# Filling the first stretch of a two-layer transformer kernel: TensorE matmuls on a tile of ones, packed inputs, a split transpose of x

## The chip, the core and the metric

The kernel runs on one core of a Trainium2 chip. A core has a matrix engine (TensorE, in the profile PE for its matmuls and PEld for its weight loads), a vector engine (VectorE, DVE), a scalar engine (ScalarE, ACT), a general engine (GpSimd, POOL) and a queue engine (SyncE, SP) that issues most of the DMAs. Each engine works through its own list of instructions in order, and waits by semaphores for the others. Matmul results land in eight PSUM banks; everything else lies in SBUF. The metric is device time in microseconds (us) for one execution; lower is better.

## The reference, cut to what matters

A row of conditions `c` makes shifts, scales and gates for every sublayer; x is 256 tokens by 1024. Two layers of three sublayers each (FFN, attention, FFN) follow:

```python
c_act = jax.nn.silu(c)
for layer in range(2):
    mod = (c_act @ ada_w[layer] + ada_b[layer]).reshape(B, 3, 3, 1024)
    h = rmsnorm(x, g) * (1 + mod[:, 0, 1]) + mod[:, 0, 0]
    x = x + 0.5 * mod[:, 0, 2] * swiglu(h, w13, w2)      # FFN, inner width 2816
    ...                                                  # attention: layer 0 windowed with sinks (swa),
    ...                                                  # layer 1 with forget gates (fox); then a second FFN
```

All inputs are float32. The modulation weights `ada_w` are 2 x 1024 x 9216 and are read whole, as are the weights of the FFNs and the projections.

## The kernel before

Precision is kept by splitting: each weight tile `wraw` (128 x 1024) is rounded on ACT to `whi` (fp32r), and DVE writes the remainder `wlo`. The activations `hT` and `gT` are split in the same way, and `mm3` issues three fast matmuls (hi*hi, hi*lo, lo*hi) for each product. The modulation `c_act @ ada_w` isn't done on PE: `cb` is silu(c) spread over all 128 partitions, and one DVE instruction (`dot`) multiplies a tile of `ada_w` with it and sums along the row.

Order on the engines is not the order of the code. A recorder keeps all operations with their dependences, and a planner (`Recorder.run`) then walks through simulated time with a cost for each operation, and takes for every engine the ready operation that is due first. DMAs have a simulated rate (343 bytes per ns in the code), matmuls a cost that doubles while the simulated TensorE clock is cold. The result is emitted as a fixed list per engine. `rec.also` gives an operation a second engine that it may be put on.

The first stretch is `start`. Conditions `c` and x are loaded, ACT takes the silu of the row `crow` (the first partition of `gate`), two matmuls with a row of ones spread it (`ps<-gate,ones`), and ACT copies the result to `cb`. `rstd` takes the sums of squares of x, `norm` scales it to `xn`, 16 transposes on PE (`ps<-ident,xn`) turn it, and ACT copies it to two tiles `xT`. Then come 8 steps, one for each 128 rows k of the first w13 matrix (`w13s`): `modulated(k)` makes two dots, shift and scale of this k, and `h`, hi and lo of `hT`; 24 matmuls (N=512) for four column chunks c follow, into all eight PSUM banks (`pa` and `ps` in the profile). The lines that spread silu(c) and the two alternatives for `h`:

```python
A.activation(crow, crow, AF.Silu)
for i in range(2):
    T.matmul(pc, ones[0:1, :], crow[:, i * 512 : i * 512 + 512], start=True, stop=True)
    A.copy(cb[:, i * 512 : i * 512 + 512], pc)
...
o = V.tensor_scalar(out=t, in0=xT[k // 4][:, k % 4, :], scalar1=mod[1][:, k : k + 1], ...)
rec.also(o, A, "activation", t, xT[k // 4][:, k % 4, :], AF.Identity, ...)
```

Small inputs come by five DMAs: `colb` and `gcol` (issued by ACT), `qkg`, `sink` and `bf` (issued by POOL, the last two spread over the partitions by the DMA). Every instruction is emitted from one helper line, so the profile's line is the same for all, and names of tiles tell them apart.

## Time and profile before

| what | us |
|---|---|
| median of 3 runs | 1003.95 (1002.23 to 1004.24) |
| the profiled execution: its own time | 1004.72 |
| its span, first to last instruction | 1002.9 |
| PE busy in the span | 981.6 (98%) |
| DVE / ACT / POOL busy | 774.7 / 522.5 / 55.3 |
| PE busy in the first 15.74 us | 7.69 |
| first split matmul of step 0 starts at | 15.74 |
| attention of layer 0, 205 to 276: PE busy | 66.36 of 71.00 |
| attention of layer 1, 680 to 790: PE busy | 106.77 of 110.00 |

PE is in use almost throughout, so a reader looks for the places where it waits: the first 15.74 us, the two attention stages and the tail. Busy time in the profile includes the pipeline's latency, so that a row of short matmuls looks fuller than it is.

### The profile page before, as it was taken

To read this page: it belongs to the slowest core of one execution; us is meant where nothing else is said; L and a number is where in the kernel's file an instruction comes from. 1 tells how busy PE (TensorE), PEld (TensorE's weight loads), DVE (VectorE), ACT (ScalarE), POOL (GpSimd) and SP (SyncE) were. 2 spreads that over 40 slices of the span, in tenths; PEclk is the share of its full clock that TensorE was granted. 3 is DMA by queue.
4 is the path that set the end of the run, shared out by engine and by line. 5 is a ranking of instruction groups with operands and counts; after the bars stand their busy time and mean duration, and the time that the engine had idled before them with its cause. 6 is when DMAs were issued, how large, how long until landed. Compare 5 with 4: busy or idle time off the path is not lost.

```text
span 1002.9 us, 16605 instructions
## 1 busy us (share of the span) xinstructions
PE 981.6 (98%) x6262; PEld 891.2 (89%) x6262; DVE 774.7 (77%) x1396; ACT 522.5 (52%) x946; POOL 55.3 (6%) x77
## 2 busy tenths in 40 slices
PE   6999999998999999999999999999999999999997
PEld 4898999897788899999889999989899789999996
DVE  5999788888999976677897767678788997555532
ACT  6473335465986543454544433447577675444420
POOL 1000000033000000000100000002211010000000
PEclk9999999999999999999999999999999999999999
DMA  9999899779446886786787878844536357656501
GB/s 344 409 354 399 332 391 308 253 269 294 148 150 253 330 316 225 318 302 237 283 315 275 311 274 306 317 157 153 166 128 249 137 191 263 212 191 240 189 33 64
DMA packets 74258, 252.92 MB, mean 252 GB/s; under 512 B 8497, under 2 KB 11969, under 8 KB 74178
## 3 DMA queue, kind: packets, MB, share of 16 engines
q1 hardware_dynamic: 73186, 249.63, 67.9%
q10 hardware_dynamic: 896, 2.21, 0.7%
q8 instruction: 49, 0.80, 0.3%
q0 software_dynamic: 96, 0.02, 0.1%
q14 instruction: 31, 0.25, 0.1%
HBM read 249.95 MB, written 1.88 MB: 251 GB/s over the span
## 4 chain that ended last, share of the span: by engine, by line
PE 91%; ACT 3%; DVE 3%; DMA 1%; POOL 1%; issue 1%; DVEq 0%; POOLq 0%
PE ps L238 57%; PE pa L238 33%; ACT t L238 1%; POOL qrs L238 1%; DVE wraw L238 1%; DMA sink<-in_sink 1%; DMA M<-foxsc 1%; DVE wlo L238 1%; ACT zeroed L238 0%; DVE qss L238 0%; DVE t L238 0%; ACT whi L238 0%; DVE qn L238 0%; ACT hT L238 0%; DVE qkv L238 0%
## 5 line engine op out<-in xcount | busy, mean ns | idle before, releaser
L238 DVE TENSOR_TENSOR wlo<-wraw,whi 128x1024 fp32r<-128x1024 f32 (+2 forms) x328 | 379.8, 1180 | 96.1 <-ACT whi L238 45.4
L238 ACT CAST whi<-wraw 128x1024 fp32r<-128x1024 f32 (+2 forms) x328 | 325.4, 1021 | 164.1 <-PE ps L238 74.5
L238 PE MATMUL ps<-hT,whi 128*128 128x256 f32 x2176 | 393.0, 283 | 0.0
L238 PEld LDWEIGHTS ps<-hT,whi 128*128 128x128 f32 x2176 | 341.0, 192 | 2.6 <-issue 0.6
L238 PE MATMUL ps<-hT,wlo 128*128 128x256 f32 x1088 | 307.7, 283 | 0.0
L238 PE MATMUL pa<-whi,gT 128*128 128x512 f32 x704 | 217.9, 391 | 0.3 <-DVE gT L238 0.3
L238 PEld LDWEIGHTS ps<-hT,wlo 128*128 128x128 f32 x1088 | 208.7, 192 | 0.0
L238 PE MATMUL ps<-whi,hT 128*128 128x384 f32 (+2 forms) x640 | 188.0, 365 | 1.4 <-DVE zeroed L238 1.4
L238 DVE SCALAR_TENSOR_TENSOR wraw<-wraw,cb 128x1024 f32<-128x1024 f32 x144 | 173.2, 1217 | 6.8 <-DMA wraw<-in_ada 6.8
L238 PEld LDWEIGHTS pa<-whi,gT 128*128 128x128 f32 x704 | 132.2, 188 | 27.7 <-DVE gT L238 0.7
L238 PE MATMUL pa<-wlo,gT 128*128 128x512 f32 x352 | 133.4, 391 | 0.0
L238 PEld LDWEIGHTS ps<-whi,hT 128*128 128x128 f32 x640 | 117.9, 189 | 12.8 <-DVE zeroed L238 1.8
L238 PE MATMUL ps<-wlo,hT 128*128 128x384 f32 (+2 forms) x320 | 116.6, 365 | 0.5 <-DVE wlo L238 0.5
L238 ACT ACTIVATE sil<-ps 128x256 f32<-128x256 f32 x84 | 31.8, 381 | 105.7 <-PE ps L238 105.7
L238 PEld LDWEIGHTS pa<-wlo,gT 128*128 128x128 f32 x352 | 66.1, 188 | 12.8
L238 PEld LDWEIGHTS ps<-wlo,hT 128*128 128x128 f32 x320 | 60.5, 189 | 6.5 <-DVE wlo L238 0.9
L238 DVE TENSOR_TENSOR sil<-sil,ps 128x256 f32<-128x256 f32 x84 | 34.6, 415 | 39.0 <-ACT sil L238 39.0
L238 ACT CAST gT<-sil 128x256 fp32r<-128x256 f32 x68 | 27.0, 405 | 61.1 <-DVE sil L238 54.2
L238 DVE TENSOR_TENSOR gT<-sil,gT 128x256 fp32r<-128x256 f32 x68 | 28.2, 421 | 18.8 <-ACT gT L238 18.8
L238 POOL TENSOR_TENSOR rs<-u,mhalf 128x1 f32<-128x1 f32 x12 | 14.5, 1209 | 484.5 <-DVE u L238 484.5
L238 PE MATMUL pa<-whi,OT 128*128 128x512 f32 x128 | 39.4, 392 | 0.0
L238 PE MATMUL pa<-zeroed 128*128 128x256 f32 x192 | 37.2, 300 | 2.2 <-ACT zeroed L238 1.8
(120 smaller groups left out, 732.2 us busy)
## 6 DMA issues: line engine op xcount, KB each, us to landing
wraw<-in_ada SPq DMA_DIRECT2D x144, 512.0 KB, 7.1
wraw<-in_w13b SPq DMA_DIRECT2D x132, 512.0 KB, 6.5
wraw<-in_w SPq DMA_DIRECT2D x88, 512.0 KB, 5.9
wraw<-in_w13a SPq DMA_DIRECT2D x28, 512.0 KB, 7.9
wraw<-in_fwin SPq DMA_DIRECT2D x28, 384.0 KB, 4.3
wraw<-in_w13s SPq DMA_DIRECT2D x16, 512.0 KB, 10.2
wraw<-in_swin SPq DMA_DIRECT2D x16, 384.0 KB, 7.2
wraw<-in_swout SPq DMA_DIRECT2D x8, 512.0 KB, 6.3
```

The lines of the kernel that those rows point to most:

```text
L238: return lambda: getattr(real, method)(*[un(v) for v in a], **{n: un(v) for n, v in k.items()})
```

## The change

Seven edits, all but one of them in the first stretch:

1. 48 filler matmuls: stationary `ones` (128 x 128), moving 64 columns of the same tile, float32, into a PSUM bank `warm` that nobody reads. The planner emits the next filler whenever PE would have nothing to issue at that moment, and they cost what its price for a float32 matmul says.
2. The simulated DMA rate goes from 343 to 400 bytes per ns, in due times and in the simulated transfers. This touches the order of the whole program.
3. The five small inputs become one tensor `small` (128 x 232), with one DMA on ACT's queue.
4. silu moves from the row to the spread copy: the matmuls take the raw `c`, and ACT applies Silu as it evacuates each half of `cb`.
5. In `start`, the sums of squares may go to DVE (`first=True`), and `xn` is always made on DVE.
6. x is transposed in two halves: columns 0 to 511 before step 0, columns 512 to 1023 inside step 0, after the first column chunk.
7. `h` of the 8 steps is made on ACT alone.

```diff
+    ones = cp.tile([P, P], F32, name="ones")
+    G.memset(ones, 1.0)
+    warm = psum()
+    rec.filler = True
+    for _ in range(NWARM):
+        T.matmul(warm[:, 0:64], ones, ones[:, 0:64], start=True, stop=True)
+    rec.filler = False
...
+                    if pick is None and e == "PE" and fillers and fillers[0].wait == 0 and t >= fillers[0].ready:
+                        o = fillers.pop(0)
+                        busy[e] = t + o.dur * (2 if cold else 1)
...
-                due = min(due, s.due - o.dur - lat(o, s) - (DMARG + o.bytes / 343 if o.bytes else 0))
+                due = min(due, s.due - o.dur - lat(o, s) - (DMARG + o.bytes / 400 if o.bytes else 0))
...
-    A.activation(crow, crow, AF.Silu)
-        A.copy(cb[:, i * 512 : i * 512 + 512], pc)
+        A.activation(cb[:, i * 512 : i * 512 + 512], pc, AF.Silu)
...
+            if first:
+                rec.also(o, V, "scalar_tensor_tensor", out=t, in0=x[h][:, c], scalar=1.0 / 1024.0, in1=x[h][:, c],
+                         op0=ALU.mult, op1=ALU.mult, accum_out=ss[:, dh : dh + 1])
...
-        xn = [norm(0), norm(1, A)]
+        rs = [rstd(h, True) for h in range(2)]
+        def transposed_x(g):
+            for h in range(2):
+                V.tensor_scalar(out=xn, in0=x[h][:, g * 512 : g * 512 + 512], scalar1=rs[h], scalar2=None, op0=ALU.mult)
+                ...
+        transposed_x(0)
...
-            o = V.tensor_scalar(out=t, in0=xT[k // 4][:, k % 4, :], ...)
-            rec.also(o, A, "activation", ...)
+            A.activation(t, xT[k // 4][:, k % 4, :], AF.Identity, scale=mod[1][:, k : k + 1], bias=mod[0][:, k : k + 1])
...
+                if k == 0 and c == 1:
+                    transposed_x(1)
```

What stands on PE from its first instruction to the first split matmul (`pa<-...`), before:

```order
L238 MATMUL ps<-gate,ones 128x512 x2
L238 MATMUL ps<-ident,xn 128x128 x16
L238 MATMUL pa<-whi,hT_212 128x512
L238 MATMUL pa<-wlo,hT_212 128x512
L238 MATMUL pa<-whi,hT_216 128x512
```

and after:

```order
L240 MATMUL ps<-ones 128x64 x8
L240 MATMUL ps<-gate,ones 128x512 x2
L240 MATMUL ps<-ones 128x64 x16
L240 MATMUL ps<-ident,xn 128x128 x4
L240 MATMUL ps<-ones 128x64 x3
L240 MATMUL ps<-ident,xn 128x128 x4
L240 MATMUL ps<-ones 128x64 x21
L240 MATMUL pa<-whi,hT_232 128x512
L240 MATMUL pa<-wlo,hT_232 128x512
L240 MATMUL pa<-whi,hT_232 128x512
L240 MATMUL pa<-wlo,hT_232 128x512
L240 MATMUL pa<-whi,hT_245 128x512 x2
```

All 48 fillers (`ps<-ones`) stand ahead of the first split matmul: 8 ahead of the spreading of c, 16 ahead of the first transposes, 3 between the two groups of transposes, 21 behind them. Eight transposes have left this place; they stand behind the sixth split matmul.

ACT's list in the same stretch, before:

```order
L238 ACT_TABLE_LOAD
L238 ACTIVATE gate<-gate 1x1024
L238 ACTIVATE t,ss<-x_94 128x512
L238 ACTIVATE t,ss<-x_99 128x512
L238 COPY cb<-ps 128x512
L238 ACTIVATE t,ss<-x_99 128x512
L238 ACTIVATE t,ss<-x_94 128x512
L238 COPY cb<-ps 128x512
L238 ACTIVATE xn<-x_99,rs 128x512 x2
L238 CAST whi<-wraw 128x1024
```

and after:

```order
L240 ACT_TABLE_LOAD
L240 ACTIVATE t,ss<-x_94 128x512
L240 ACT_TABLE_LOAD
L240 ACTIVATE cb<-ps 128x512 x2
L240 COPY xT<-ps 128x4x128
L240 CAST whi<-wraw 128x1024
L240 COPY xT<-ps 128x4x128
L240 ACTIVATE h_226<-xT,mod_203,mod_187 128x256
L240 CAST hT_232<-h_226 128x256
L240 CAST whi<-wraw 128x1024
L240 COPY xT<-ps 128x4x128 x2
L240 CAST whi<-wraw 128x1024 x2
```

Three of the four squares and both `xn` have gone to DVE, a second table load stands ahead of the two Silu, and the copies of the second half of `xT` stand ahead of the casts of step 1's weights.

Beyond the first stretch PE's list differs in the attention of layer 0 (205 to 276 us of the profile). Around its first scores (`ps<-qkv`; `ident,kn` and `ident,qn` are transposes of normalised keys and queries), before:

```order
L238 MATMUL ps<-qkv 128x128 x3
L238 MATMUL ps<-qkv 128x256 x3
L238 MATMUL ps<-whi,hT_2185 128x384
L238 MATMUL ps<-qkv 128x128 x3
L238 MATMUL ps<-qkv 128x256 x3
L238 MATMUL pa<-ident,kn 128x128
L238 MATMUL pa<-ident,qn 128x128 x2
L238 MATMUL ps<-wlo,hT_2185 128x384
```

and after:

```order
L240 MATMUL pa<-ident,qn 128x128 x2
L240 MATMUL pa<-ident,kn 128x128
L240 MATMUL ps<-whi,hT_2269 128x384
L240 MATMUL ps<-wlo,hT_2269 128x384
L240 MATMUL ps<-whi,hT_2309 128x384
L240 MATMUL ps<-qkv 128x128 x3
L240 MATMUL ps<-qkv 128x256 x3
L240 MATMUL ps<-qkv 128x128 x3
L240 MATMUL ps<-qkv 128x256 x3
L240 MATMUL ps<-whi,hT_2244 128x384
```

The transposes that stood right behind the first scores now stand ahead of them, with projection matmuls (`ps<-whi,hT`) between.

## The prediction, made before the changed kernel ran

> **What bounds the kernel now.** I read the page's busy shares first, then a table of windows by stage, then the chain that ended last.

> ```profile
> PE 981.6 (98%) x6262; PEld 891.2 (89%) x6262; DVE 774.7 (77%) x1396; ACT 522.5 (52%) x946; POOL 55.3 (6%) x77
> 0.00:15.74 15.74, 7.69 (x20) 4.30 (x20) 5.33 (x15) 11.28 (x21) 4.37 (x15) 1.00 0.88 306
> 15.74:23.02 7.28, 7.28 (x25) 5.89 (x26) 7.28 (x12) 5.01 (x7) 0.00 (x0) 1.00 1.02 407
> 23.02:61.10 38.08, 38.08 (x170) 31.53 (x170) 36.37 (x66) 17.97 (x27) 0.00 (x0) 1.00 1.03 409
> 61.10:205.00 143.90, 143.90 (x962) 132.50 (x962) 123.73 (x187) 68.05 (x104) 1.72 (x2) 1.00 0.91 336
> 205.00:276.00 71.00, 66.36 (x423) 58.94 (x422) 64.52 (x193) 50.04 (x146) 19.61 (x30) 0.98 0.67 226
> ```

> A window's row gives its length and the busy time of PE, PEld, DVE, ACT and POOL, then the granted clock. PE never stops from 15.74 to 205 us. So what the first stretch gains or loses is carried to 205 unchanged, provided DVE and the DMAs (GB/s in the last column) keep up; and PE idles 8.05 us (15.74 - 7.69) ahead of it. The chain shows what filled that time.

> ```profile
> 2.41 6.77 DMA sink<-in_sink
> 12.74 1.07 ACT xT L238 x2
> 15.74 4.53 PE pa L238 x12
> 20.28 2.74 PE ps L238 x12
> 23.02 2.72 PE pa L238 x12
> 55.66 2.72 PE pa L238 x12
> ```

> A slow small DMA (sink, 6.77 us) held DVE's list, behind which stood rstd; then xn, transposes, xT, h. Step 0 is 24 matmuls: the first 12 took 4.53 us, the next 2.74, all later dozens 2.72, or 0.227 each. The first stretch therefore ends at 23.02 for step 0, and every later step costs 5.44.

> **The clock.** PE's rows show why the first dozen is slow.

> ```profile
> 4.14 3.75 PE L238 MATMUL ps<-gate,ones 1*128 1x512 f32 x4 [4.14 <-ACT gate L238]
> 10.95 2.82 PE L238 MATMUL ps<-ident,xn 128*128 128x128 f32 x12 [3.06 <-ACT xn L238]
> 18.04 1.05 PE L238 MATMUL pa<-whi,hT 128*128 128x512 f32 x2
> 18.90 0.46 PE L238 MATMUL pa<-wlo,hT 128*128 128x512 f32 x1
> 237.00:238.00 1.00, 0.50 (x2) 0.42 (x2) 1.00 (x3) 0.99 (x4) 1.00 (x1) 0.74 1.14 259
> 238.00:239.00 1.00, 1.00 (x4) 1.00 (x4) 1.00 (x4) 0.44 (x2) 0.69 (x2) 0.50 0.75 164
> 241.00:242.00 1.00, 1.00 (x9) 0.77 (x7) 1.00 (x2) 0.97 (x3) 0.62 (x1) 1.00 0.98 393
> ```

> Up to 18.90 two matmuls take 0.86 us from start to start, 0.43 each; the one at 18.90 is already shorter, and the later dozens take 0.227 each. So the clock doubles at about 19.0, 3.3 us after full matmuls began. The granted clock column says 1.00 there and doesn't show this early half clock; at 237.5 it does show a fall to 0.50, for some 3.4 us. Neither the 3.75 us on c (one row of the array) nor the transposes raised it.

> **The fillers.** Each is a float32 matmul with a full stationary tile. The nearest rows are three such instructions with 16 moving columns, at full clock:

> ```profile
> 702.34 0.74 PEld L238 LDWEIGHTS ps<-lf,tri 128*128 128x128 f32 x6
> L238 PEld LDWEIGHTS ps<-lf,tri x6: 187/192/192, 702.3 to 702.9; 128*128 128x128 f32 x6
> 211.10 1.03 PE L238 MATMUL ps<-ident,xn 128*128 128x128 f32 x8
> 211.89 0.42 PE L238 MATMUL ps<-whi,hT 128*128 128x384 f32 x1
> 0.74 0.20 POOL L238 MEMSET ones<- 128x128 f32 x1 [0.29 <-POOLq L1272]
> ```

> Three instructions make six weight loads and six matmuls; the loads start (0.74 - 0.19)/5 = 0.11 us apart. So a filler (two of each) is 0.22 us at full clock, 0.44 at half. That is a lower bound as 64 columns stream longer than 16; if loads and matmuls didn't overlap it would be about 0.33. I take 0.22, since weight loads overlap the matmuls everywhere else (PE 98% and PEld 89% busy). Eight transposes take 0.79 (211.10 to 211.89), the spreading of c half of 3.75, or 1.88, all at full clock. PE's list up to the first split matmul is then 48 x 0.22 + 1.88 + 0.79 = 13.23 us at full clock. It can start at 1.0, when `ones` is written. If the clock rises at time w, the part before w runs at half speed, so the first split matmul starts at S = 1.0 + 13.23 + (w - 1.0)/2.

> For w the earliest is 1.0 + 3.3 = 4.3 (fillers count like full matmuls). The first 8 fillers last 8 x 0.44 = 3.5 us, to 4.5, and then come the matmuls on c, of the kind that didn't raise the clock before. I take 6.0, nearer to the early end as the fillers use all 128 rows, and later than 4.3 because that 3.75 us stretch shows that length alone isn't enough. S = 16.73.

> [...]

> **Is anything later than PE's list?**

> ```profile
> 1.64 1.28 ACT L238 ACT_TABLE_LOAD   x1 [1.64 <-PEq L1272]
> 4.85 0.63 ACT L238 ACTIVATE t<-x 128x512 f32<-128x512 f32 x1 [0.85 <-DMA x<-in_x]
> 6.79 0.63 ACT L238 ACTIVATE t<-x 128x512 f32<-128x512 f32 x1 [1.22 <-DMA x<-in_x]
> 9.57 1.09 POOL L238 TENSOR_TENSOR rs<-u,mhalf 128x1 f32<-128x1 f32 x2 [5.38 <-DVE u L238]
> 12.24 1.22 DVE L238 SCALAR_TENSOR_TENSOR wraw<-wraw,cb 128x1024 f32<-128x1024 f32 x1
> 14.64 0.61 ACT L238 ACTIVATE h<-xT,mod,mod 128x256 f32<-128x256 f32 x1
> 15.29 0.40 ACT L238 CAST hT<-h 128x256 fp32r<-128x256 f32 x1
> 16.59 1.05 ACT L238 CAST whi<-wraw 128x1024 fp32r<-128x1024 f32 x1
> ```

> x lands at 4.85 and 6.79; two squares on DVE (half of 1.22 each) end at 8.0, rs (0.55) at 8.8, two xn at 9.6. PE's 8 fillers end at 4.52, c's matmuls run at half clock to 6.0 and need (3.75 - 1.48)/2 = 1.14 more, to 7.14, and 16 fillers end at 10.7: the transposes don't wait. ACT: square to 5.6, the added table load (1.28) to 6.9, two Silu like the copies of xT (0.53 each), done by 8. The table load is hidden under x and c; without that cover it would cost its 1.28. Dots 2 x 1.15 from 9.6 end at 11.9, shift and scale 12.2, second xT copy 12.7, h and hT 13.8. So the data are ready near 14 and wait for PE: 21 fillers of 0.22 (4.6 us) stand ahead of them. The packing removes the sink wait (up to 9.2), and one DMA on ACT's queue replaces five on two; both gains end in the same wait for PE's list, so I count them as zero.

> **Step 0 and the later steps.** Step 0 lasts 24 x 0.227 + 0.79 for the moved transposes = 6.23, and ends at 16.73 + 6.23 = 22.96, against 23.02: -0.06. The two moved xn come on DVE before the second `wlo`; ACT's xT copies wait for the transposes, and behind them are queued the casts of step 1 and its h.

> ```profile
> 24.91 0.41 DVE L238 TENSOR_SCALAR h<-xT,mod,mod 128x256 f32<-128x256 f32 x1
> 27.90 1.22 DVE L238 SCALAR_TENSOR_TENSOR wraw<-wraw,cb 128x1024 f32<-128x1024 f32 x1
> 33.49 1.22 DVE L238 SCALAR_TENSOR_TENSOR wraw<-wraw,cb 128x1024 f32<-128x1024 f32 x1
> 11.47 1.61 SPq L238 DMA_DIRECT2D wraw<-in_w13s  x2
> 14.04 1.61 SPq L238 DMA_DIRECT2D wraw<-in_ada  x2
> ```

> Transposes end near 19, copies 20, two casts of 1.05 at 22, h and hi 22.9: just ahead of step 1 at 22.96. DVE needs 5.59 us per step (27.90 to 33.49), more than PE's 5.44; without h (0.33 to the next start) it needs 5.26. So edit 7 earns nothing by itself, but keeps DVE ahead. Lo of hT now stands behind both `wlo`, and I add 0.2 for stalls in steps 2 and 3 (0 to 0.5). A pair of tiles is issued every 2.57 us, a step's four in 5.14, less than 5.44: DMAs don't bind.

> **The attention of layer 0** is reordered by edit 2; its waits are these:

> ```profile
> 236.19 0.33 PE L238 MATMUL pa<-ident,kn 128*128 128x128 f32 x1 [0.62 <-ACT kn L238]
> 237.58 0.69 PE L238 MATMUL ps<-wlo,hT 128*128 128x384 f32 x1 [0.50 <-DVE wlo L238]
> 248.37 0.44 PE L238 MATMUL ps<-whi,hT 128*128 128x384 f32 x1 [1.45 <-DVE zeroed L238]
> ```

> With kn's and qn's transposes now ahead of the scores, the waits of 0.62 and 0.50 can go, and the clock's fall behind them. DVE (64.52 of 71.00) limits that gain. I take half of 1.12, -0.56; bounds are -3 (both waits, 1.45, and part of the slow clock) and +2 (the same size in new waits). The rest of the program keeps PE's order: 0.

> The sum: -0.06 + 0.2 - 0.56 = -0.4 us, on the profiled execution 1004.72 to 1004.3, on the median 1003.95, 0.77 below it, to 1003.5. About 0.2%, or 2 us, is what a measurement of this kernel can tell from no change.

> **The rivals.**

> 1. The clock rises late: slower. If c's matmuls interrupt the count, it starts anew in the second batch, at 4.52 + 3.75 = 8.3, and w is 11.6 or later, 13 with some delay: S = 20.2, step 0 ends at 26.5, 3.5 later than in the forecast: 1007.0. It decides from w = 10.8, where S is 2.4 us later and the sum reaches +2. If fillers never count, all runs at half clock: S = 1.0 + 26.5 = 27.5, step 0 as before 7.28 plus 1.6 for the transposes at half clock, 36.4 against 23.02: 1017. For it: two kinds of PE work did not raise the clock. Against: fillers use all rows, as the matmuls at 15.74 do.

> 2. Attention recovers more: faster. If the fall of the clock at 237.5 doesn't come back, 3.4 us at half speed give up to 1.7 us, and with the waits of 1.12 -2.8 in place of -0.56: 1001.3. For it: the chain ran over those matmuls on PE. Against: DVE and ACT are the fuller engines behind them.

> 3. Fillers are cheaper than their nearest row, say 0.14 us: PE's list shrinks by 48 x 0.08 = 3.8, data decide at 14, step 0 ends at 20.2 in place of 22.96: 1000.8. Against: 0.11 is the tightest spacing of float32 loads in the trace.

> **How the numbers follow.** Forecast, within 2 us of before: 0.39. Late clock: 0.27 (never: 0.06 of it). Attention: 0.22. Cheap fillers: 0.12. Faster by over 0.2% is the last two, 0.34; same 0.39; slower 0.27. The predicted time is 1003.5; alone it would range from 1001.9 to 1005.9. As both signs hold most of the chance, the range reaches below rivals 2 and 3 by 1 us, the unknown rest of the attention, and 1.5 above the late clock: 999.8 to 1008.5. It leaves out the clock that never rises.

> **What would show it.** PE's rows: `ps<-ones` 0.22 apart at full and 0.44 at half clock, no idle PE from 1.0 to the first `pa<-whi,hT`, which starts near 16.7 with `hT` ready near 14. First dozen of step 0 in 2.72 plus the transposes. The chain should run over `ones` on PE, not over `sink`. In the attention the granted clock should stay nearer to 1.00. Fillers 0.44 apart throughout, or a first split matmul past 18.7, would make it wrong; so would one before 15.

## The result, and the profile after

The changed kernel takes 1014.46 us (median of 10 runs, 1007.29 to 1017.81), the kernel before 1004.11 in the same session (median of 10, 1002.23 to 1009.77). The ratio is 1.0088, 95% interval 1.0066 to 1.0110: slower by 0.9% (the two medians alone would give 1.0%). The forecast was 1003.5, its range 999.8 to 1008.5.

The profiled execution took 1017.2 us, with a span of 1015.3. First the page's busy times, then the table of windows by stage (length; busy PE, PEld, DVE, ACT, POOL; granted clock; DMA share; GB/s):

```profile
PE 1002.8 (99%) x6358; PEld 913.6 (90%) x6358; DVE 779.1 (77%) x1408; ACT 521.8 (51%) x934; POOL 49.8 (5%) x74
0.00:26.89 26.89, 25.90 (x109) 23.24 (x109) 12.37 (x30) 8.55 (x12) 2.65 (x12) 1.00 0.94 372
26.89:34.58 7.69, 7.69 (x34) 6.28 (x34) 1.64 (x3) 4.32 (x7) 0.00 (x0) 1.00 1.03 411
34.58:72.66 38.08, 38.08 (x169) 31.42 (x168) 37.64 (x64) 23.86 (x36) 0.00 (x0) 1.00 0.88 333
```

PE is busier than before (1002.8 against 981.6 us) and the kernel is slower: the added 21 us are about what 48 fillers take at the 0.43 us that one costs in the rows below. PE has no gap from 0.99 to the first split matmul at 26.89, which before started at 15.74. Behind step 0 little has changed: PE has no gap in the 38.08 us that follow, as before, and from step 1 to the chain's first long block of 288 matmuls (its rows stand in the section on the planner's rate) it is 125.16 us, before 125.10. The chain that ended last (start, length, what) says where the time went in three rows:

```profile
0.99 26.14 PE ps L240 x108
27.13 2.63 PE pa L240 x6
34.74 2.72 PE pa L240 x12
```

The six split matmuls of the second row take 0.44 us each, the twelve of the third 0.227: half clock, then full clock. Step 1 starts at 34.74, before at 23.02, both by the chain: 11.72 us later. The rest of the span is 980.56 us against 979.88, 0.68 more. So all but 0.68 of the 12.4 us by which the span has grown lies ahead of step 1. PE's timeline shows what stands there (start, length, tile, count of records; a filler leaves two):

```profile
0.99 3.68 PE L240 MATMUL ps<-ones 128*128 128x64 f32 x16 [0.99 <-POOL ones L240]
4.60 3.78 PE L240 MATMUL ps<-gate,ones 1*128 1x512 f32 x4
8.30 7.09 PE L240 MATMUL ps<-ones 128*128 128x64 f32 x32
15.19 1.06 PE L240 MATMUL ps<-ident,xn 128*128 128x128 f32 x4
16.04 1.38 PE L240 MATMUL ps<-ones 128*128 128x64 f32 x6
17.21 1.06 PE L240 MATMUL ps<-ident,xn 128*128 128x128 f32 x4
18.07 9.06 PE L240 MATMUL ps<-ones 128*128 128x64 f32 x42
26.89 0.77 PE L240 MATMUL pa<-whi,hT 128*128 128x512 f32 x1
```

The 21 fillers behind the transposes take 8.82 us to the next row's start, 0.42 each; the 16 ahead of them 6.89, 0.43 each. That is the price at half clock from the first to the last. The clock rose only at 29.6 us, 2.7 us after the split matmuls began. And the fillers were not in idle time. The planner's price for one is 64 x 1.667 + 30 = 137 ns, doubled while its own clock is cold; it took some 430, so the list that fits the plan's idle time does not fit the chip's. ACT's timeline shows the copy of xT waiting 7.28 us for PE, whose transposes stood behind fillers, and hT cast at 19.56, done at 19.97. PE could not start on it for another 6.9 us.

```profile
16.28 0.58 ACT L240 COPY xT<-ps 128x512 f32<-128x512 f32 x1 [7.28 <-PE ps L240]
19.56 0.41 ACT L240 CAST hT<-h 128x256 fp32r<-128x256 f32 x1
```

The wait on `sink` is gone, as the packing intended, but nothing shows of it under the fillers.

### The profile page after: what moved, and what is told of

It is laid out like the page before. It is cut to its first block, busy times and chain, and to the rows that moved or that the text cites. A ratio compares the mean times of both kernels' runs of the same rounds, so it can differ in the third digit from the quotient of the medians.

```text
span 1015.3 us, 16811 instructions
## 1 busy us (share of the span) xinstructions
PE 1002.8 (99%) x6358; PEld 913.6 (90%) x6358; DVE 779.1 (77%) x1408; ACT 521.8 (51%) x934; POOL 49.8 (5%) x74
## 3 DMA queue, kind: packets, MB, share of 16 engines
HBM read 249.96 MB, written 1.88 MB: 248 GB/s over the span
## 4 chain that ended last, share of the span: by engine, by line
PE 94%; ACT 2%; DVE 2%; DMA 1%; POOL 0%; issue 0%; DVEq 0%; POOLq 0%; ACTq 0%
PE ps L240 61%; PE pa L240 34%; DMA M<-foxsc 1%; ACT whi L240 1%; ACT t L240 1%; POOL qrs L240 0%; DVE t L240 0%; DMA wraw<-in_w13b 0%; DMA wraw<-in_swin 0%; ACT zeroed L240 0%; DVE zeroed L240 0%; DVE wraw L240 0%; DVE qn L240 0%; DVE qss L240 0%; ACT kn L240 0%
## 5 line engine op out<-in xcount | busy, mean ns | idle before, releaser
L240 DVE SCALAR_TENSOR_TENSOR wraw<-wraw,cb 128x1024 f32<-128x1024 f32 x144 | 173.1, 1218 | 12.5 <-DMA wraw<-in_ada 12.4
L240 PEld LDWEIGHTS pa<-wlo,gT 128*128 128x128 f32 x352 | 66.2, 188 | 12.8
L240 PE MATMUL pa<-zeroed 128*128 128x256 f32 x192 | 39.8, 315 | 2.7 <-ACT zeroed L240 1.8
L240 PEld LDWEIGHTS pa<-zeroed 128*128 128x128 f32 x192 | 31.2, 201 | 6.5 <-ACT zeroed L240 3.0
## 6 DMA issues: line engine op xcount, KB each, us to landing
wraw<-in_w13s SPq DMA_DIRECT2D x16, 512.0 KB, 10.2
```

The costliest lines, as they stand in the source:

```text
L240: return lambda: getattr(real, method)(*[un(v) for v in a], **{n: un(v) for n, v in k.items()})
```

## Experiments

"Rise" and "fall" below are times of the trace's record of the granted clock. The record begins with the first rise, so the clock column of a view says 1.00 ahead of it too; there the matmuls' own times tell. In the trace of before the stretches between two changes are 218.45, 3.41 and 761.17 us, in that of the changed kernel 232.11, 10.24, 457.39, 3.41 and 283.31: each a whole multiple of 3.413 us (64, 1 and 223; 68, 3, 134, 1 and 83). (The last stretch, which the end of the run cuts off, is left out.) At half clock the other traces fit: 6.83 and 13.65 us in e6_nofill_343, 10.24 in e1_no_fillers. I call a stretch of 3.41 us a window. Windows on the time ahead of the first rise are counted back from it, an estimate of mine from these multiples.

### The change without fillers, and with wider ones

```diff
-NWARM = 48
+NWARM = 0
```

> The change without its 48 fillers; all else stays. Both theories say that the fillers, 0.42 us each at half clock, hold PE's list to 26.9 us without raising the clock. Without them the data decide: hT near 14 us by the prediction's sum of rows, then step 0 with its moved transposes (24 x 0.227 + 0.79 = 6.2 us at full clock) and 1.7 to 3.4 us lost at half clock, so step 1 begins at 21.9 to 23.6 us in place of 34.6. Total 11 to 12.7 us below the profiled run of the changed kernel, 1002 to 1005 us. If the rest of the change were itself to blame for the loss, it would stay above 1010.

1001.62 us, ratio 0.9971 (0.9954 to 0.9987). PE waits 2.25 us for hT, starts at 13.41, and step 1 starts at 21.50, 1.52 us earlier than before, although the first matmuls run at half clock, 0.43 us apart (rise at 16.55). Both the start of step 1 and the time lie a little below what was expected. PE's timeline and the chain:

```profile
13.41 0.79 PE L240 MATMUL pa<-whi,hT 128*128 128x512 f32 x1 [2.25 <-ACT hT L240]
21.50 2.72 PE pa L240 x12
```

So the rest of the change is a gain of 0.3%, and the 48 fillers cost 12.8 us between the medians.

```diff
-        T.matmul(warm[:, 0:64], ones, ones[:, 0:64], start=True, stop=True)
+        T.matmul(warm[:, 0:128], ones, ones, start=True, stop=True).dur = 64 * 1.667 + 30
```

> Fillers of 128 moving columns in place of 64, with the planner's price for one left as it was, so the count stays 48. The weight loads set the spacing (0.33 us busy for a load and 0.42 for a matmul at half clock), so a filler should cost 0.43 to 0.5 us at half clock, but stream twice as many columns per us. Theory A (the clock rises by the share of time in which columns are streamed): it rises 3.4 to 7 us after the fillers' start, at 4.4 to 8 us, the fillers fall to 0.22 to 0.25 us, the first split matmul starts at 16 to 18 us and step 1 at 22.5 to 24: 1003 to 1006 us. Theory B (float32 matmuls on a constant tile never count, however wide): no rise before the split matmuls have run for some 3 us, fillers 0.43 or more throughout, first split matmul at 27 us or later, 1014 us or more.

1004.77 us, ratio 1.0001 (0.9983 to 1.0019): the 48 fillers twice as wide cost 9.7 us less than the narrow ones, between the medians. PE's timeline, and its windows between the clock's changes:

```profile
0.99 3.79 PE L240 MATMUL ps<-ones 128*128 128x128 f32 x16 [0.99 <-POOL ones L240]
4.70 1.98 PE L240 MATMUL ps<-gate,ones 1*128 1x512 f32 x4
6.61 5.02 PE L240 MATMUL ps<-ones 128*128 128x128 f32 x28
11.91 4.63 PE L240 MATMUL ps<-ones 128*128 128x128 f32 x40
18.94 0.48 PE L240 MATMUL pa<-whi,hT 128*128 128x512 f32 x1
4.65:8.06 3.41, 3.41 (x18) 2.11 (x18) 2.51 (x8) 3.09 (x5) 0.55 (x1) 1.00 1.02 414
8.06:11.48 3.42, 3.42 (x19) 3.42 (x18) 3.12 (x9) 0.00 (x0) 1.47 (x1) 0.50 1.02 416
```

The first 16 records take 3.7 us to the next row's start, the narrow ones 3.6: at half clock 64 more columns are nearly free. Behind the first, the records of fillers start 0.213 us apart with 64 columns and with 128, and so do their weight loads, which are the same; so it is not the columns that set this pace. I take it to be the weight loads (PEld is busy for 3.42 of 3.42 us from 8.06 to 11.48), which no run shows by itself. The clock rises at 4.65, so c's four matmuls take 1.98 in place of 3.78. B falls: the clock rose 3.66 us after the first of the float32 matmuls on ones, with nothing else run on PE. It falls again at 8.06, at the end of a window with PE busy for all of its 3.41 us, 1.9 of them on c's matmuls of one row; it rises again at 11.48 and stays up to the attention of layer 0 (40 records then take 4.46 to the next row's start, 0.22 a filler). The first split matmul starts at 18.94, and step 1 at 24.66, both later than in A (16 to 18, and 22.5 to 24), for these 3.4 us at half clock.

### The type of the filler, and the planner's rate

```diff
+    onesr = cp.tile([P, P], F32R, name="onesr")
+    G.memset(onesr.bitcast(F32), 1.0)
...
-        T.matmul(warm[:, 0:64], ones, ones[:, 0:64], start=True, stop=True)
+        T.matmul(warm[:, 0:64], onesr, onesr[:, 0:64], start=True, stop=True).dur = 64 * 1.667 + 30
```

> Fillers on a tile of ones of the split matmuls' type (fp32r), still 64 columns and 48 of them, with the planner's price left as it was. Theory A (share of time with streamed columns): one pass in place of two leaves the share low, so the clock does not rise before the split matmuls; a filler takes some 0.2 to 0.27 us at half clock and the list of 48 ends at 18 to 21 us in place of 26.9; step 0 begins at half clock; 1007 to 1010 us. Theory B (float32 matmuls don't count, fp32r ones do): the clock rises at 4.4 to 8 us and fillers fall to 0.11 to 0.14 us, the data decide from 14 us, step 1 begins at 20.2 to 21.5: 1000.5 to 1003 us.

1006.55 us, ratio 1.0020 (1.0003 to 1.0037): half a microsecond below A's 1007 to 1010, and far from B's 1000.5 to 1003.

```profile
12.07 4.88 PE L240 MATMUL ps<-onesr 128*128 128x64 f32 x22
16.77 0.78 PE L240 MATMUL pa<-whi,hT 128*128 128x512 f32 x1
```

One record per filler, 4.70/22 = 0.21 us each, no rise before the split matmuls (at 20.14). So the first split matmul starts at 16.77, earlier than A's 18. Behind fillers of the split matmuls' own type the clock did not rise either, though from 13.31 to 16.72, a whole window, PE ran nothing else.

```diff
-                due = min(due, s.due - o.dur - lat(o, s) - (DMARG + o.bytes / 400 if o.bytes else 0))
+                due = min(due, s.due - o.dur - lat(o, s) - (DMARG + o.bytes / 343 if o.bytes else 0))
-                        dma = max(dma, t + 1100) + max(o.bytes / 400, 60)
+                        dma = max(dma, t + 1100) + max(o.bytes / 343, 60)
```

> The planner's two divisors for a DMA's bytes back from 400 to 343; all else as in the changed kernel, fillers too. It tells what the changed order in the attention is worth apart from the first stretch. The profiled execution lost 11.6 us up to step 1 and 0.8 us behind it, while the clock stood at half for 10.2 us in the attention of layer 0. If the new order there is what brings the slow clock, the time from step 1 to the end falls from 980.7 to 979.9 us or less, and the whole by 0.5 to 2 us; if the slow clock there comes by chance of where the clock's windows lie, no difference over 0.2%. Either way the first stretch ends at 34 to 36 us and the time is 1012 to 1017 us.

1016.45 us, ratio 1.0125 (1.0106 to 1.0144; four runs). It shows the narrow fillers in another position of the windows:

```profile
8.30 8.37 PE L240 MATMUL ps<-ones 128*128 128x64 f32 x38
19.35 4.41 PE L240 MATMUL ps<-ones 128*128 128x64 f32 x36
23.59 0.61 PE L240 MATMUL ps<-ident,xn 128*128 128x128 f32 x4
```

The last 36 records take 4.24 us, 0.236 a filler, for the clock rose at 19.93, among the fillers; behind the rise it is 0.22. The window that ended there, from 16.51, held both groups of transposes (1.67 us) with the fillers between; in the changed kernel's trace a window began at 15.92, in the midst of the first group, and did not rise. The windows of 64-column fillers alone (three in the changed kernel's trace) never did. Step 1 starts at 30.14, not at the 34 to 36 that I had expected, and the rest takes 981.96 us, more than the 980.56 of the changed kernel: the new order behind step 1 is not what loses. Where the clock's windows fall on this list seems to matter for the changed kernel too. Five of its ten executions have a mean granted clock of 0.998, so about one window of half clock behind the first rise, and yet take 1007.29 to 1014.08 us; without fillers the three at 0.998 take 999.04 to 1000.28. That spread would lie ahead of the first rise, but there is a trace of one execution alone.

The same edit without fillers:

```diff
 (the change with NWARM = 0)
-  o.bytes / 400   (both places)
+  o.bytes / 343
```

> The change without fillers and with the planner's divisor back at 343: beside the kernel without fillers (1001.62 us) it tells what the other divisor is worth where the fillers don't blur it. If the new order in the attention is the gain (my sum put it at 0.56 us, with bounds from a gain of 3 to a loss of 2), this runs at 1002 to 1004 us; if the gain of the kernel without fillers is all in the first stretch (step 1 at 21.3 in place of 23.0), it stays within 0.5 us of 1001.6.

1003.35 us, ratio 1.0003 (0.9982 to 1.0025), beside 0.9954 to 0.9987 at 400, and within the 1002 to 1004 expected if the new order is a gain. Step 1 starts at 21.49, the same; so the 1.7 us between the medians lie in the order behind it. The intervals just overlap, and this trace is of the slowest of twelve executions, so it takes more traces to say it. In each trace the chain has four blocks of 288 matmuls; the first two enclose the attention of layer 0. Rows of the chain of before, of the changed kernel, and of the kernel with x transposed whole, told of below, in which TensorE's matmuls stand in the same order here as in the changed kernel:

```profile
148.12 34.55 PE ps L238 x288
436.48 34.55 PE ps L238 x288
```

```profile
159.90 34.55 PE ps L240 x288
447.31 34.55 PE ps L240 x288
```

```profile
144.94 34.55 PE ps L240 x288
430.04 34.55 PE ps L240 x288
```

From block to block: 288.36 us before, 287.41 after, 285.10 in the third. What differs on TensorE between the last two is the half clock, 10.24 us of it in the changed kernel's attention, 3.41 in the third kernel's. All traces, by TensorE's order in this stretch:

| planner's rate and order | half clock in this stretch | block to block, us |
|---|---|---|
| 343, before | 3.41 | 288.36 |
| 343, e4_rate343 and e6_nofill_343, one order | 3.41 and 20.48 | 288.50 and 296.20 |
| 400, the changed kernel's order: after, e1, e3, e5 | 10.24 | 287.41 to 287.55 |
| 400, the same order: e7, e9, e11 | 3.41 | 284.93 to 285.10 |
| 400, an order of its own: e2_n128 | 6.83 | 285.91 |
| 400, two orders of their own: e8, e10 | 3.41 | 283.56, 283.53 |

With 3.41 us at half clock the changed kernel's order is 3.3 to 3.4 us shorter than before's, and two others at 400 are 4.8 shorter. In the changed kernel's order 6.83 us more of half clock cost 2.3 to 2.6 us, so some 1.2 us a window.

### Which matmuls the clock rose behind

Fillers as transposes of the tile of ones, 48 of them:

```diff
-        T.matmul(warm[:, 0:64], ones, ones[:, 0:64], start=True, stop=True)
+        T.transpose(warm[:, 0:128], ones, ident).dur = 64 * 1.667 + 30
```

> The 48 fillers are transposes of the tile of ones (ident is made first, so they start near 2 us), at the same price in the planner. They stand as tight on TensorE as the transposes of xn, 0.21 us each at half clock, 48 of them some 10 us. Theory A1 (transposes count like other streaming matmuls): a window full of them raises the clock, by 12 us at the latest since c's one-row matmuls end near 7.5; transposes then take 0.11 us, the first split matmul starts at 14 to 16 us, step 1 at 20.5 to 22.5, and the time is 1000.5 to 1003 us. Theory A2 (transposes don't count): they stay at 0.21 us, the first split matmul starts at 17.5 to 19 us, the clock rises some 3 us later, and the time is 1005 to 1008 us.

1001.02 us, ratio 0.9969 (0.9956 to 0.9982): A1.

```profile
3.18 3.78 PE L240 MATMUL ps<-gate,ones 1*128 1x512 f32 x4
6.89 3.15 PE L240 MATMUL ps<-ident,ones 128*128 128x128 f32 x14
11.19 2.67 PE L240 MATMUL ps<-ident,ones 128*128 128x128 f32 x23
13.95 0.50 PE L240 MATMUL pa<-whi,hT 128*128 128x512 f32 x1
```

Ahead of the rise at 9.82 lies a window of 0.49 us of c's matmuls and 2.93 of nothing but transposes, 0.21 each; behind it they take 0.12. A2 falls: the clock rose behind transposes, these of float32.

c spread over 128 rows, with 20 wide fillers:

```diff
-NWARM = 48
+NWARM = 20
...
+    V.memset(gate, 0.0)
+    row0 = cp.tile([P, P], F32, name="row0")
+    G.memset(row0, 0.0)
+    G.memset(row0[0:1], 1.0)
...
-        T.matmul(warm[:, 0:64], ones, ones[:, 0:64], start=True, stop=True)
+        T.matmul(warm[:, 0:128], ones, ones, start=True, stop=True).dur = 232
...
-        T.matmul(pc, ones[0:1, :], crow[:, i * 512 : i * 512 + 512], start=True, stop=True)
+        T.matmul(pc, row0, gate[:, i * 512 : i * 512 + 512], start=True, stop=True)
```

> 20 fillers of 128 columns, and the spreading of c done over 128 rows in place of one: c's tile is set to zero by VectorE ahead of its DMA, and the weights are a tile with ones in row 0 and zeros below. The matmuls on c cost the same; the DMA of c now lies behind x and one tile of weights. If it is the one row that keeps (or brings back) the half clock, as in the kernel with 48 wide fillers, where the clock rose at 4.65 us, fell at 8.06 behind c's matmuls and rose again at 11.48, the clock now rises at 4.4 to 8 us and does not fall; step 1 begins at 18.7 to 21 us, and the time is 998 to 1000.5 us. If rows don't matter, the clock falls again behind c's matmuls and the time is 1000.5 to 1003 us.

1000.71 us, ratio 0.9966 (0.9953 to 0.9979), 0.2 us above what was expected.

```profile
7.53 1.95 PE L240 MATMUL ps<-gate,row 128*128 128x512 f32 x4 [0.87 <-DMA gate<-in_c]
13.96 0.50 PE L240 MATMUL pa<-whi,hT 128*128 128x512 f32 x1 [1.17 <-ACT hT L240]
5.84:9.25 3.41, 2.54 (x11) 1.45 (x11) 2.91 (x10) 2.59 (x4) 1.48 (x2) 1.00 1.02 413
```

The clock rises at 5.84 and stays, through a window in which PE was busy for only 2.54 of 3.41 us. With one row it fell after a window busy throughout (e2_n128, at 8.06). So idle time in the window was not what brought the clock down there; I put the difference down to c's matmuls, of one row there and of 128 here. The 127 rows that were added hold nothing but zeros. Step 1 starts at 19.56 by PE's rows; the data (hT, a wait of 1.17) now set the start, later here because c's DMA lies behind x.

Twelve wide fillers at an honest price, so that the planner puts them only where PE idles:

```diff
-NWARM = 48
+NWARM = 12
-        T.matmul(warm[:, 0:64], ones, ones[:, 0:64], start=True, stop=True)
+        T.matmul(warm[:, 0:128], ones, ones, start=True, stop=True).dur = 464
```

> The change with 12 fillers of 128 columns in place of 48 of 64, each at a price in the planner (0.46 us) that is what one takes at half clock, so that they lie only where TensorE would idle (3 ahead of c's matmuls, 4 behind them, 1 between the two groups of transposes, 4 ahead of the first split matmul). Theory A (the clock follows the share of time in which columns stream over many rows): c's one-row matmuls keep the clock low until 6.5 us, then fillers and transposes fill one window, and the clock rises between 9.8 and 13.4 us in place of 16.5 without fillers; step 1 begins 1 to 2.5 us earlier than there (21.3), the time is 999 to 1001 us. Theory B (the fillers only delay; the split matmuls alone raise the clock): the fillers stand in front of the transposes and of the split matmuls by up to 1 us and nothing is gained: 1001.5 to 1003 us.

998.00 us, ratio 0.9937 (0.9919 to 0.9955), a microsecond below A's 999 to 1001. The interval just touches that of the kernel without fillers (0.9954 to 0.9987).

```profile
6.28 2.08 PE L240 MATMUL ps<-ones 128*128 128x128 f32 x8
10.30 1.27 PE L240 MATMUL ps<-ones 128*128 128x128 f32 x8
12.67 0.50 PE L240 MATMUL pa<-whi,hT 128*128 128x512 f32 x1 [1.10 <-ACT hT L240]
19.33 2.72 PE pa L240 x12
```

The rise comes at 10.75, after a window that held transposes and wide fillers alone. PE then waits 1.10 us for hT and starts step 0 at full clock: step 1 at 19.33, 3.7 us earlier than before, 2.2 earlier than without fillers.

The same with 32 columns:

```diff
-        T.matmul(warm[:, 0:128], ones, ones, start=True, stop=True).dur = 464
+        T.matmul(warm[:, 0:32], ones, ones[:, 0:32], start=True, stop=True).dur = 464
```

> The kernel with 12 fillers at the same places and the same price, with 32 moving columns in place of 128: the spacing stays at about 0.43 us at half clock, since the weight loads set it, and TensorE is as busy. Theory A (streamed columns raise the clock): a window that held nothing but transposes and wide fillers (7.34 to 10.75 us there, full) now streams for some 0.6 of its length, no more than windows that have not raised the clock in any trace so far (up to 0.66); so it rises only behind the split matmuls, at 15 to 19 us, step 1 begins at 20.5 to 22.5 us in place of 19.17, and the time is 1000.5 to 1003 us. Theory C (it is TensorE's being busy without a gap, not the columns, that counts, and the 48 fillers of 64 columns failed for another reason): the clock rises as with 128 columns, at 9.8 to 13.4 us, and the time is 997.5 to 999.5 us.

1000.60 us, ratio 0.9966 (0.9951 to 0.9980). The two intervals just touch; the traces differ plainly.

```profile
6.28 1.92 PE L240 MATMUL ps<-ones 128*128 128x32 f32 x8
11.78 1.75 PE L240 MATMUL ps<-ones 128*128 128x32 f32 x8
14.25 0.80 PE L240 MATMUL pa<-whi,hT 128*128 128x512 f32 x1 [0.72 <-ACT hT L240]
10.06:13.47 3.41, 3.41 (x18) 3.33 (x16) 3.39 (x8) 2.43 (x4) 0.00 (x0) 1.00 1.03 416
23.71 2.72 PE pa L240 x12
```

Eight records take 1.92 us against 2.08, so PE is about as busy, and from 10.06 to 13.47, one window of the clock, it is never idle: 1.43 us of transposes and 1.98 of these fillers. The clock does not rise there. With 128 columns it rose after a window of 1.73 us of transposes and 1.69 of fillers. C falls: both windows were busy throughout, and the clock rose behind the one with 128 columns alone.

The rise comes at 20.30, behind the split matmuls, later than A's 15 to 19, and step 1 starts at 23.71, 4.4 us behind the kernel with 128 columns and later than A's 22.5. Not all of that is the width. In this execution the second tile of x landed later, as DVE's first squares of it show (128 columns, then 32):

```profile
6.10 0.69 DVE L240 SCALAR_TENSOR_TENSOR t<-x 128x512 f32<-128x512 f32 x1 [0.23 <-DMA x<-in_x]
7.68 0.69 DVE L240 SCALAR_TENSOR_TENSOR t<-x 128x512 f32<-128x512 f32 x1 [1.89 <-DMA x<-in_x]
```

These 1.58 us are those between the first split matmuls (12.67 and 14.25). The execution is also the slowest of twelve, six of which took 998.29 to 1000.05 us, so the clock may not rise as late in all of them.

### Two more parts of the change, on the kernel with 12 wide fillers

```diff
         transposed_x(0)
+        transposed_x(1)
...
-                if k == 0 and c == 1:
-                    transposed_x(1)
```

> The kernel with 12 wide fillers, with both halves of x transposed ahead of step 0 (edit 6 undone). Two xn more on VectorE (0.52 us each in the kernel with 12 fillers) can come ahead of the dots that the first split matmul waits for; step 0 loses its eight transposes (0.79 us). If the first split matmul waits for data, it starts at 13.2 to 13.9 us in place of 12.67, and step 1 at 18.7 to 19.4 in place of 19.17: no difference over 0.2% from 998.0 us. If the split is what the gain hangs on, step 1 starts past 20.2 and the time is above 999.5 us.

998.14 us, ratio 0.9944 (0.9931 to 0.9957): no difference from 998.00. The first split matmul starts at 14.15, 1.5 us later (both halves of xn come ahead of it), and step 1 at 19.86 against 19.33, since step 0 is free of the transposes; both a little later than expected. The split of x is worth half a microsecond at the start of step 1 in these two traces, and nothing that the medians show.

```diff
-            A.activation(t, xT[k // 4][:, k % 4, :], AF.Identity, scale=mod[1][:, k : k + 1], bias=mod[0][:, k : k + 1])
+            V.tensor_scalar(out=t, in0=xT[k // 4][:, k % 4, :], scalar1=mod[1][:, k : k + 1],
+                            scalar2=mod[0][:, k : k + 1], op0=ALU.mult, op1=ALU.add)
```

> The kernel with 12 wide fillers, with h of the 8 steps on VectorE in place of ScalarE (edit 7 undone, and forced). By my sum VectorE then needs 5.59 us a step against TensorE's 5.44, so the steps stall on VectorE for some 0.15 us each, 1 us from step 1 to the eighth, and up to 2 where the first steps have no lead: 998.5 to 1000.5 us. If VectorE keeps ahead by its lead, no difference from 998.0 us.

996.77 us, ratio 0.9935 (0.9921 to 0.9949), the best of all, though not told apart from 998.00. I had expected a loss. DVE's timeline, same operation in two steps:

```profile
20.45 1.22 DVE L240 SCALAR_TENSOR_TENSOR wraw<-wraw,cb 128x1024 f32<-128x1024 f32 x1
25.87 1.22 DVE L240 SCALAR_TENSOR_TENSOR wraw<-wraw,cb 128x1024 f32<-128x1024 f32 x1
```

With h on it DVE needs 5.42 us a step, not 5.59, and PE 5.44. From step 1 to the first block of 288, by PE's rows, it is half a microsecond slower (19.75 to 145.61, against 19.17 to 144.49), which is lost among larger differences in the attention (3.41 us of half clock here, 10.24 in the profiled execution of the other, and another order of TensorE's matmuls). h on ScalarE buys nothing that shows in the time.

## Why the prediction was wrong, point by point

**The step that failed** is the choice of w = 6.0, "nearer to the early end as the fillers use all 128 rows". No run shows a rise near 6.0 behind these fillers: the profiled execution had w = 29.6. Rows mattered (behind c's matmuls the clock fell at 8.06 with one row, and held with 128), but all 128 were not enough: with 64 columns the clock stayed at half, with 128 columns it rose at 4.65, although eight fillers take 3.6 us with 64 and 3.7 with 128. Nor was it that c's matmuls interrupt the count, as rival 1 had it: the 16 fillers behind them ran for 6.89 us without a break, and the clock stayed down. The sum lacked the question whether the width of a filler matters, and the row it rested on led to it: I had priced the filler at 0.22 from matmuls of 16 columns, so by my own sum the width did not set the spacing. That 64 columns stream for too small a share of it is theory A; the runs show widths and rises, not the array itself. The branch in which fillers never count was then given 0.06 and left out of the range.

In two traces one window of wide fillers was enough: the clock rose at 4.65 (e2_n128) and 5.84 (e8_rows128), 3.7 and 4.5 us after the first filler. The fillers of this change kept PE busy through whole windows, three with nothing but fillers, without a rise. The prediction also read from the rows of before that the transposes had not raised the clock; the rise at 9.82 in e7_transposes came behind transposes of float32. Before, they had simply not filled a window: 12 of them in 2.82 us.

**The sum's other terms held.** PE's list is 13.23 us at full clock in the sum; at half clock it ran from 0.99 to 26.89, which is 12.95 at full. The filler's 0.22 and 0.44 came out at 0.22 (wide, full clock) and 0.43. The formula for S, with fillers that never count, gave 27.5: measured 26.89. That branch put the end of step 0 at 36.4, measured 34.74, since the clock rose at 29.6, 2.7 us into the split matmuls; its time of 1017 stands against 1017.2 profiled and 1014.46 in the median. The near hit on 1017.2 is luck: the end of step 0 was 1.7 us off, and the profiled execution is the second slowest of ten.

**"The transposes don't wait"** fell with w: at half clock they started at 15.19 in place of 10.7. "Data ready near 14" was right for the kernel without fillers (hT let PE start at 13.41).

**Packing, counted as zero** because both its gains end in the wait for PE's list: right for this kernel. Its worth may show with the fillers gone, as part of the 1.5 us by which step 1 then comes earlier. I did not test it apart from the new placing of the squares and xn.

**Stalls of 0.2 us in steps 2 and 3**: none over 0.07. **Edit 7 earns nothing by itself**: so it came out on the kernel with 12 wide fillers, though DVE's 5.59 was too high.

**The attention's -0.56** came out at -0.95 in this trace, block to block, but as a sum of larger parts: some 3.3 us gained by the order at the same half clock, 2.4 of it lost again to 6.83 us more of half clock there. The fall of the clock was not removed, as rival 2 had it, but made longer. Elsewhere the rest gave +0.95 (second to third block: 188.38 before, 189.33 after; the other kernels at 400 have 189.3 to 189.5, the two others at 343 188.3, so the other rate costs a microsecond there), +1.50 (third to fourth, with one more window of half clock), -0.88 at the end and +0.06: 0.68 in all. I had put the rest of the program at zero.

**Not settled**: how much of a window must be filled for the clock to rise. Windows with 0.81 and 0.85 of their length in transposes and wide fillers did not rise (the kernels with h on DVE, with x whole), one with 0.86 did (transposes, 2.93 of 3.42 us); these lie too close together to give a limit. If 0.86 is taken as what was needed, a 64-column filler would have to stand for some 0.7 of its time in the window that rose at 19.93 (1.67 us of transposes, 1.75 of fillers), and for less than 0.8 in the changed kernel's that began at 15.92 and did not rise (0.98 and 2.44). Yet 64 columns are half of 128, and eight fillers take 3.6 us with the one and 3.7 with the other, so by theory A the share would be no more than about 0.5: theory A is not the whole of it either. These are estimates from a few windows.

## What to carry to other kernels

Here filler matmuls paid when they were wide and few: against no fillers, 12 of 128 columns brought step 1 forward by 2.2 us, and 48 of 64 put it back by 13.2. With 64 columns eight fillers took 3.6 us against 3.7 with 128, PE looked 100% busy, and the clock stayed at half up to 29.6. Price fillers at the clock they will run at, and put in no more of them than the wait holds. When a sum hangs on one switch such as the rise of a clock, give the branch in which it doesn't switch a chance, and its time a place in the range.

## What the hardware showed that I had not expected

- A busy PE was not enough for the clock to rise. Behind a window of 3.41 us with no idle PE it did not (e11_n32, 32-column fillers), behind one with 0.49 us of one-row matmuls and 2.93 of transposes it did (e7_transposes), and it fell after a window busy throughout (e2_n128, 1.9 us of it on one-row matmuls) but held through one with 0.87 us idle and all rows (e8_rows128).
- Widening a float32 filler from 64 to 128 columns was nearly free at half clock (3.68 and 3.79 us for eight) and at full clock (0.22 each for both, behind the rise in e4_rate343 and e2_n128).
- The half clock lasted in the attention: once it had fallen PE was the busiest engine (in the changed kernel's window below 13.07 of 15.00 us, at a mean clock of 0.66), and with matmuls all along the clock stayed down for up to four windows (13.65 us in e6_nofill_343, PE busy for all of them; 10.24 in the changed kernel).
- How much half clock there is differs between executions of one kernel, and the time with it: the six of the kernel with 12 wide fillers go from a mean granted clock of 0.993 and 1001.85 us to 1.000 and 995.35.

```profile
260.00:275.00 15.00, 13.07 (x70) 11.39 (x71) 10.54 (x50) 10.82 (x38) 2.17 (x7) 0.66 0.28 111
```
